# A RWKV scan in double periods: the triangular solver moved to GpSimd one period ahead, and transfers, norms and weight splits set in another order

## The chip, the core and the metric

The kernel runs on one core of a Trainium2 chip. A core has five engines with a queue each: PE (TensorE, matrix multiplication), DVE (VectorE), ACT (ScalarE), POOL (GpSimd) and SP (SyncE, which here only starts DMA transfers). The metric is the device time of one execution in microseconds (us). Before the change three runs gave 2839.25, 2841.23 and 2844.28 us; the median is 2841.23.

## What is computed

A decoder trunk of two layers over 272 tokens (16 learned ones and 256 of the input) with 2048 channels, in float32. Layer 0 mixes tokens by RWKV-7 with 32 heads of 64 channels, then has a SwiGLU block; layer 1 has stick-breaking attention and another SwiGLU block. The change touches layer 0's mixing alone:

```python
r = xr @ w_r;  k = xk @ w_k;  v = xv @ w_v
w = -softplus(-(dec_w0 + tanh(xw @ dec_w1) @ dec_w2)) - 0.5
decay = exp(-exp(w))
a = sigmoid(a_w0 + (xa @ a_w1) @ a_w2)
g = sigmoid(xg @ g_w1) @ g_w2
kk = heads(k * k_k);  kk = kk * rsqrt(max(sum(kk * kk), 1e-24))
k = k * (1 + (a - 1) * k_a)
def step(state, inp):                       # one token, for each head
    sa = einsum('bhvk,bhk->bhv', state, -kk_t)
    state = state * d_t + sa * (kk_t * a_t) + v_t * k_t
    return state, einsum('bhvk,bhk->bhv', state, r_t)
y = group_norm(y) * gn_w + gn_b             # over each head
out = ((y + sum(r * k * r_k) * v) * g) @ w_o
```

## The kernel before

**Stages.** `prologue` normalizes the tokens, computes all of k and the hidden layers of the low-rank products, and prepares the mixed inputs of r and v. `scan` (L662) runs the recurrence and, beside it, the projections of r and v and the first part of the output projection. The SwiGLU blocks and the attention follow; they are not touched.

**Pairs and chunks.** Two heads make a pair of 128 channels; there are 16 pairs. A pair's 272 tokens are a chunk of 16 and four chunks of 64. Within a chunk the recurrence is a triangular system, so a chunk needs the inverse of a unit triangular 64 x 64 matrix built from the scores `An` (L1323). The inverse is made in two stages. First its 16 x 16 diagonal blocks: the scores go to a DRAM scratch `s1` (L1308), from where a transfer picks the diagonals of two pairs into `As` on 80 partitions (`diagonals`, L826); `solve` (L832) inverts them all by 14 steps of two DVE operations; `inverse` (L848) writes the result `Ts` to a scratch `s2` and reads it back as the tile `Tt`. Then `left` and `right` (L1382, L1405) double the blocks, once for size 16 and once for 32, by TensorE. `apply`, `trans` and `states` (L1420, L1436, L1456) turn the inverse into chunk transitions, and `step` (L1471) walks through the four chunks.

**The double period.** `scan` works on two pairs at a time, in turn d = -2 to 7. In each turn, A is the pair of pairs at its end (states, steps, group norm, gate), B the one in its middle (scores, inverse, transitions), and C the one at its start: `lora` (L1199) makes decays and the scaled key tensors of one pair from the low-rank products. N is the one behind C, for which weights are loaded. In one turn, the order before the change is: A's states and steps with B's `neg` and `chunk0` between them; B's scores and `diagonals`; `bonus`, `tokens`; A's norm, one pair after the other; `solve`; C's first `lora`; `values`; A's gates; `inverse`; left 16, C's second `lora`, right 16, left 32, right 32, apply, trans.

**Fill.** Between these parts stand calls `f(k)`: they draw k steps from `stream` (L902), each three matmuls of 272 columns for the r and v projections (w_v before w_r; 64 steps per turn). The weights come in 512 KB tiles `raw` on SyncE's queue (four buffers), are split into `whi` by ACT and `wlo` by DVE in parts of 512 columns, four steps each (`whl_pair`, L222; six buffers), and `chunks` (L857) splits one part ahead of its use.

**Order.** TensorE's and SyncE's instructions keep the order of the program text. For the other engines the framework's scheduler orders them by its own estimate of when operands are ready, unless the text pins an instruction: `in_step` (L820), `issue_after` and the manual dependencies in `chunks` do so before the change. Each engine runs its queue in order, and a wait holds up all behind it.

**Queues.** `self.dq` (L391) gives pair 0 of a turn SyncE's queue for its scratch transfers, and pair 1 GpSimd's. `load_low` and `split_low` (L788, L802) load and split the small second-stage weights: one pair's decay weights together with another pair's gate weights, and with the former the tile `rn`, the reciprocal norms of the keys. GpSimd computes most of `lora`'s products (`E` in L1202), among them kk, the product of the keys with `rn`.

**Buffers.** `BUFS` (L54) lists how many buffers a tag has; a tag that is not listed has one, and `ALIAS` (L38) lets two names share a tag.

Of the kernel before, what the change touches and what calls it, by code (L numbers as in the profile page):

```python
# [18 lines left out]
NK = D // 128  # L19
# [18 lines left out]
ALIAS = {"kk": "ld", "rs2": "L", "rk": "Q", "Ah": "Tn", "Mp": "Ys", "sq": "ta"}  # L38
# [15 lines left out]
BUFS = {n: 2 for n in "ARV BK AR0 G An Tt X BV0 Tn Ys Rh S KV0 WV0 y bv hs rn".split()}  # L54
BUFS.update(bv=3, pe=6)

# [75 lines left out]
class Builder:  # L132
# [240 lines left out]
    def time_mix(self):  # L373
# [15 lines left out]
        with ExitStack() as ctx:  # L389
            sp = ctx.enter_context(tc.tile_pool(name="sp", bufs=1, reuse_waits="tile"))  # L390
            self.dq = nc.sync, nc.gpsimd  # L391
            self.static = []
            self.s2 = []
# [3 lines left out]
            for i in range(2):  # L397
                st = {}
                for n, w in (("B0", 64), ("V0", 64), ("SC0", 128)):
                    st[n] = sp.tile([128, w], F32, name=f"{n}_{i}", tag=f"{n}_{i}")  # L400
                    nc.gpsimd.memset(st[n], 0.0)
                self.static.append(st)
                z = self.dram.tile([10, 65, 64], F32, name=f"s2_{i}", tag=f"s2_{i}", bufs=1)
                nc.scalar.dma_start(z.rearrange("s i t -> (s i t)").rearrange("(p x) -> p x", p=128),
                                  zero)
                self.s2.append(z)
# [255 lines left out]
    def scan(self, sp):  # L662
# [24 lines left out]
        self.load_low(None, pairs[0])  # L687
        for d in range(-2, NK // 2):
            A, B, C, N = two(d), two(d + 1), two(d + 2), two(d + 3)
            f = fill if C else lambda k: fill(k * 7 / 8)  # L690
            self.split_low(nth(A, 0), nth(C, 0), self.latest)
            self.load_low(nth(A, 1), nth(C, 1))
            if d == -2:
                C[0].lora(4, 5)
                f(12)
                pop, head_sq, key_max, key_norm = self.late_keys
                head_sq(*pop())
                late = key_max(1)
                f(28)
                self.split_low(None, C[1], self.steps[-1])  # L700
                self.load_low(None, N[0])
                C[1].lora(0, 1)
                f(24)
                continue
# [3 lines left out]
            for c in range(1, 5):  # L708
                for x in A:
                    x.step(c)  # L710
                if not B:
                    fill(1)
                elif c < 3:
                    B[c - 1].neg()
                elif c == 3:
                    if not A:
                        f(6)
                    for x in B:
                        x.chunk0()
# [5 lines left out]
            if B:  # L725
                B[0].bonus()
            for x in B:
                x.tokens()
            if A:
                A[0].square()  # L730
                A[0].variance()
            f(2)
            if A:
                A[0].norm()
            if B:
                B[1].bonus()
            if A:
                A[1].square()
            f(2)
            if A:  # L740
                A[1].variance()
            f(2)
            with tc.issue_after(self.solve(B).ins) if B else nullcontext():
                if A:
                    A[1].norm()
                if C:
                    C[0].lora(2, 3)
                f(4)
                if A or C:
                    self.split_low(nth(A, 1), nth(C, 1), self.steps[-1])  # L750
                    self.load_low(nth(B, 0), nth(N, 0))
                f(4)
                for x in B:
                    x.values()
                f(4)
                if A:
                    A[0].gate()
                f(4)
                if A:
                    A[1].gate()  # L760
                f(6 if A else 4)
            if B:
                self.inverse(B)
            for x in B:
                x.left(16)
            f(5)
            if C:
                C[1].lora(0, 1)
            for x in B:
                x.right(16)  # L770
            f(5)
            for x in B:
                x.left(32)
            f(5)
            for x in B:
                x.right(32)
            if d == -1:
# [10 lines left out]
    def load_low(self, A, C):  # L788

        if not (A or C):  # L790
            return
        nc, a = self.nc, self.a
        self.low = self.l2.tile([128, 512], F32, name="w2", tag="w2", bufs=2)
        if C:
            p = C.p
            nc.sync.dma_start(self.low[:, :256], a["lora2"][p][:, :256])
            C.rn = C.t272("rn")
            nc.sync.dma_start(C.rn, self.rkd[2 * p:2 * p + 2].unsqueeze(1).to_broadcast([2, 64, T]))
        if A:
            nc.sync.dma_start(self.low[:, 256:], a["lora2"][A.p][:, 256:512])  # L800

    def split_low(self, A, C, after):  # L802
        c = slice(0 if C else 256, 512 if A else 256)
        h = self.l2.tile([128, 512], F32R, name="w2h", tag="w2h", bufs=1)
        l = self.l2.tile([128, 512], F32R, name="w2l", tag="w2l", bufs=1)
        hi = self.nc.scalar.copy(h[:, c], self.low[:, c])
        if after:
            nosync = mybir.DependencyInfo(mybir.DependencyClass.NoSync, mybir.DependencyReason.DATA)
            self.tc.add_manual_dep(hi.ins, after.ins.name, nosync,
                                   reason="weights that land late")  # L810
        self.nc.vector.tensor_tensor(l[:, c], self.low[:, c], h[:, c].bitcast(F32), ALU.subtract)
        for x, o, r in (C, 0, 96), (A, 256, 128):
            if x:
                x.w2 = [(h[:r, i:i + 128], l[:r, i:i + 128]) for i in (o, o + 128)]
# [5 lines left out]
    def in_step(self, op):  # L820

        nosync = mybir.DependencyInfo(mybir.DependencyClass.NoSync, mybir.DependencyReason.DATA)
        self.tc.add_manual_dep(op.ins, self.steps[-1].ins.name, nosync,
                               reason="operands that land late")

    def diagonals(self, two):  # L826

        self.As = self.sp.tile([80, 16, 16], F32, name="As", tag="As")
        for i, x in enumerate(two):
            self.dq[i].dma_start(self.As[i * 40:i * 40 + 40], x.diag(x.s1))  # L830

    def solve(self, two):  # L832
# [4 lines left out]
        self.in_step(V.tensor_tensor(Ts.rearrange("p i t -> p (i t)"), As.rearrange("p i t -> p (i t)"),  # L837
                                     self.cst("eye16")[:80], ALU.add))
        for i in range(1, 15):
            n = 15 - i  # L840
            t = Tm[:, :i * n].rearrange("p (i t) -> p i t", t=n)
            V.tensor_tensor(t, Ts[:, 0:i, i:i + 1].to_broadcast([80, i, n]),  # L842
                            As[:, i:i + 1, i + 1:].to_broadcast([80, i, n]), ALU.mult)
            op = V.tensor_tensor(Ts[:, 0:i, i + 1:], Ts[:, 0:i, i + 1:], t, ALU.add)  # L844
        self.Ts = Ts
        return op

    def inverse(self, two):  # L848
        for i, x in enumerate(two):
            self.dq[i].dma_start(x.diag(self.s2[i]), self.Ts[i * 40:i * 40 + 40])  # L850
        for i, x in enumerate(two):
            x.Tt = x.big("Tt", 5, 64)
            s2 = self.s2[i].rearrange("(a r) i t -> r i a t", r=2)
            for r in range(2):
                self.dq[i].dma_start(x.Tt[HS[r]], s2[r, 0:64])

    def chunks(self, jobs):  # L857
# [17 lines left out]
        nosync = mybir.DependencyInfo(mybir.DependencyClass.NoSync, mybir.DependencyReason.DATA)  # L875
        count = [0]
        self.steps = []
# [693 lines left out]
```

## Time and profile before

| what | us |
|---|---|
| median of three runs | 2841.23 |
| the profiled execution | 2843.48 |
| its span, first to last instruction | 2841.7 |
| TensorE busy | 2671.2 (94%) |
| VectorE busy | 1802.2 (63%) |
| ScalarE busy | 1491.4 (52%) |
| GpSimd busy | 211.7 (7%) |

The page's strip cuts the span into 40 slices of 71 us and gives the busy share of each engine in tenths. The stretches outside the scan show 9 for TensorE; the scan lies in slices 3 to 11. Matmul records are pipelined and overlap, so a busy TensorE is not one at its peak; how far apart matmuls start tells more. A row of a timeline has the start, the duration, engine, line, operation, and in brackets the idle time before and what ended it. A row of the waits has the total, the count and the longest.

### The profile page before, as it was taken

What the parts mean: (1) busy time and instruction counts of PE and PEld (TensorE: products, weight loads), DVE (VectorE), ACT (ScalarE), POOL (GpSimd) and SP (SyncE); (2) the same over time, 40 slices, a digit from 0 to 9 for tenths busy, and PEclk for the clock granted to TensorE, in tenths of its full rate; (3) what the DMA queues carried; (4) which work ended last, traced back from release to release, by engine and by line L of the source; (5) the groups of instructions that cost most, each with busy time, mean ns of one, the idle gap of its engine ahead of it and who ended that gap; (6) DMA issues with size and microseconds to landing.
All of it is one profiled execution on the core that took longest, in us unless ns stands there. A gap on an engine that the chain in (4) does not pass through costs nothing.

```text
span 2841.7 us, 54127 instructions
## 1 busy us (share of the span) xinstructions
PE 2671.2 (94%) x20966; PEld 2494.3 (88%) x20966; DVE 1802.2 (63%) x3689; ACT 1491.4 (52%) x3016; POOL 211.7 (7%) x301
## 2 busy tenths in 40 slices
PE   9987677768799999999999999999999999999999
PEld 8887667667699999999999999988888888888888
DVE  7665445556566555555555777578876666666666
ACT  7764443445465444444444576467655455455554
POOL 0033233333200000000000000000000000000000
PEclk9998888888899999999999999999999999999999
DMA  6442322232445555555555555543455565655655
GB/s 228 129 118 76 83 83 70 74 83 68 119 149 173 173 176 179 162 188 176 166 186 173 164 183 167 175 148 116 148 186 188 178 199 178 199 187 177 201 182 175
DMA packets 168146, 439.57 MB, mean 155 GB/s; under 512 B 38544, under 2 KB 70704, under 8 KB 167888
## 3 DMA queue, kind: packets, MB, share of 16 engines
q1 hardware_dynamic: 164240, 429.62, 48.1%
q0 software_dynamic: 3072, 5.53, 0.9%
q8 instruction: 164, 2.69, 0.4%
q10 hardware_dynamic: 576, 0.96, 0.1%
q14 instruction: 94, 0.77, 0.1%
HBM read 430.28 MB, written 5.74 MB: 153 GB/s over the span
## 4 chain that ended last, share of the span: by engine, by line
PE 87%; DMA 4%; DVE 3%; POOL 2%; ACT 2%; issue 1%; SPq 1%; DVEq 0%; POOLq 0%; ACTq 0%
PE mm L204 21%; PE mm L199 15%; PE mm L201 15%; PE mm L200 15%; PE mm L203 11%; DMA s<-Ts 2%; PE lr L598 1%; PE mm L499 1%; POOL k L1227 1%; DVE Tm L842 1%; DVE Ts L844 1%; PE yb L1394 1%; DMA Tt<-s 1%; PE zb L1410 1%; PE wa L1427 1%
## 5 line engine op out<-in xcount | busy, mean ns | idle before, releaser
L181 DVE TENSOR_TENSOR wlo<-raw,whi 128x512 fp32r<-128x512 f32 (+1 forms) x1432 | 968.2, 679 | 593.2 <-ACT whi L180 575.0
L180 ACT CAST whi<-raw 128x512 fp32r<-128x512 f32 (+1 forms) x1432 | 870.0, 610 | 839.6 <-PE mm L200 528.0
L199 PE MATMUL mm<-hl,whi 128*128 128x272 f32 x3328 | 975.7, 293 | 0.2 <-ACT whi L227 0.2
L200 PE MATMUL mm<-hl,whi 128*128 128x272 f32 x3328 | 969.3, 291 | 5.0 <-DVE hl L271 5.0
L201 PE MATMUL mm<-hl,wlo 128*128 128x272 f32 x3328 | 970.6, 292 | 0.2 <-DVE wlo L228 0.2
L204 PE MATMUL mm<-hl,whi 128*128 128x512 f32 x2624 | 919.7, 394 | 0.0
L203 PE MATMUL mm<-hl,wlo 128*128 128x256 f32 x2624 | 738.0, 282 | 0.0
L200 PEld LDWEIGHTS mm<-hl,whi 128*128 128x128 f32 x3328 | 642.5, 193 | 5.5 <-DVE hl L271 5.4
L199 PEld LDWEIGHTS mm<-hl,whi 128*128 128x128 f32 x3328 | 637.2, 191 | 5.1 <-issue 0.5
L201 PEld LDWEIGHTS mm<-hl,wlo 128*128 128x128 f32 x3328 | 636.8, 191 | 0.7 <-DVE wlo L228 0.4
L204 PEld LDWEIGHTS mm<-hl,whi 128*128 128x128 f32 x2624 | 492.4, 188 | 111.9
L203 PEld LDWEIGHTS mm<-hl,wlo 128*128 128x128 f32 x2624 | 494.3, 188 | 0.3
L227 ACT CAST whi<-raw 128x512 fp32r<-128x512 f32 (+1 forms) x154 | 92.5, 612 | 186.1 <-PE mm L200 119.1
L228 DVE TENSOR_TENSOR wlo<-raw,whi 128x512 fp32r<-128x512 f32 (+1 forms) x154 | 113.3, 754 | 110.6 <-ACT whi L227 107.3
L1394 PE MATMUL yb<-Tt,An 64*64 64x64 f32 x512 | 28.7, 260 | 84.4 <-DMA Tt<-s 84.2
L1394 PEld LDWEIGHTS yb<-Tt,An 64*64 64x64 f32 x512 | 24.3, 169 | 88.8 <-issue 79.3
L220 DVE TENSOR_TENSOR h<-h,mm 128x256 f32<-128x256 f32 (+1 forms) x224 | 93.9, 420 | 6.6 <-PE mm L204 6.0
L201 PE MATMUL mm<-hi,wlo 128*128 128x272 f32 x256 | 77.2, 302 | 21.1 <-DVE wlo L228 21.1
L199 PE MATMUL mm<-hi,whi 128*128 128x272 f32 x256 | 78.8, 308 | 0.0
L213 ACT COPY c<-mm 128x256 f32<-128x256 f32 x104 | 38.8, 373 | 76.0 <-PE mm L204 76.0
L200 PE MATMUL mm<-lo,whi 128*128 128x272 f32 x256 | 75.8, 296 | 0.0
L201 PEld LDWEIGHTS mm<-hi,wlo 128*128 128x128 f32 x256 | 50.6, 198 | 22.6 <-DVE wlo L228 22.6
(303 smaller groups left out, 2502.3 us busy)
## 6 DMA issues: line engine op xcount, KB each, us to landing
raw<-w_gate SPq DMA_DIRECT2D x176, 512.0 KB
raw<-w_up SPq DMA_DIRECT2D x176, 512.0 KB
raw<-w_down SPq DMA_DIRECT2D x128, 512.0 KB
raw<-w_down SPq DMA_DIRECT2D x128, 192.0 KB
raw<-w_v SPq DMA_DIRECT2D x32, 512.0 KB
raw<-w_r SPq DMA_DIRECT2D x32, 512.0 KB
raw<-sb_w_k SPq DMA_DIRECT2D x32, 512.0 KB
raw<-sb_w_v SPq DMA_DIRECT2D x32, 512.0 KB
```

The costliest lines, as they stand in the source:

```text
L180: nc.scalar.copy(hi, part)
L181: nc.vector.tensor_tensor(lo, part, hi.bitcast(F32), ALU.subtract)
L199: mm(out, w[0], x[0], start=first, stop=False)
L200: mm(out, w[0], x[1], start=False, stop=False)
L201: return mm(out, w[1], x[0], start=False, stop=last)
L203: mm(out[:, :n], w[1], x[0], start=first, stop=False, skip_group_check=True)
L204: return mm(out, w[0], x[2], start=False, stop=last, skip_group_check=True)
L213: self.nc.scalar.copy(c, out[:, n:])
L220: self.nc.vector.tensor_tensor(h, h, out[:, c:c + n], ALU.add)
L227: self.cast = nc.scalar.copy(hi, part)
L228: nc.vector.tensor_tensor(lo, part, hi.bitcast(F32), ALU.subtract)
L1394: PE.matmul(yb[r, i * 64:i * 64 + 64], An[r, i], Tt[r, i], start=True, stop=True)
```

## The change

- The scratch transfers of both pairs go on SyncE's queue (`self.dq`); `s1` becomes a fixed pair of tiles, zeroed once, like `s2`.
- `neg` moves to a new place, behind right 32, and works for C, the pairs that are B in the next turn. It also computes chunk 0's negative scores, into a new tile `An0`. Behind it, in the new function `negatives`, stand `diagonals`, which now writes `An` and `An0` (the scores in transposed form) to `s1`, and `solve`, which runs on GpSimd, over a transposed view of `As`, in 15 steps of two operations on a copy of the identity.
- `inverse` stands behind B's `tokens`; A's `square`, `variance`, the new `log` and `norm` follow for both pairs together.
- `lora` of both C pairs uses banks 2 and 3 and stands at other places. kk and the four products with it move from GpSimd to DVE, as fused operations.
- `load_low` and `split_low` serve the two pairs of C; `load_gates` and `split_gates` those of A. `rn` gets its own `load_norm` and has one buffer; `bv` has four.
- w_r comes before w_v. Parts are split three ahead (`AHEAD`), each cast from the 13th on pinned behind what the text has put on ACT before it. `step` is cut into `update` and `output`.

The order of the turn, cut to its core:

```diff
-            self.split_low(nth(A, 0), nth(C, 0), self.latest)
-            self.load_low(nth(A, 1), nth(C, 1))
+            gates = self.load_gates(A)
+            if C:
+                self.split_low(C)
             for x in A:
                 x.states()
             for c in range(1, 5):
                 for x in A:
-                    x.step(c)
+                    x.update(c)
+                for x in A:
+                    x.output(c)
-                elif c < 3:
-                    B[c - 1].neg()
+                elif c < 3:
+                    B[c - 1].chunk0()
             for x in B:
                 x.scores()
-            if B:
-                self.diagonals(B)
             f(6 if A else 2)
+            for x in B:
+                x.bonus()
             for x in B:
                 x.tokens()
-            (A[0] square, variance, f(2), norm; B[1].bonus; A[1] the same)
-            with tc.issue_after(self.solve(B).ins) if B else nullcontext():
-                (A[1].norm, C[0].lora, splits and loads, values, gates)
             if B:
                 self.inverse(B)
+            for x in A:
+                x.square()
+            for x in A:
+                x.variance()
+            for x in A:
+                x.log()
+            for x in A:
+                x.norm()
+            f(4)
+            if C:
+                C[0].lora(2, 3)
+            f(4)
             for x in B:
                 x.left(16)
             f(5)
-            if C:
-                C[1].lora(0, 1)
             for x in B:
                 x.right(16)
+            for x in B:
+                x.values()
+            if C:
+                C[1].load_norm()
             f(5)
+            if C:
+                C[1].lora(2, 3)
+            f(5)
+            self.split_gates(gates, A)
+            f(4)
+            for x in A:
+                x.gate()
             for x in B:
                 x.left(32)
-            f(5)
+            f(7)
             for x in B:
                 x.right(32)
+            if C:
+                self.negatives(C)
-            f(5)
+            f(8)
             for x in B:
                 x.apply()
-            f(5)
+            if N:
+                self.load_low(N)
+                N[0].load_norm()
+            f(8)
             for x in B:
                 x.trans()
-            f(5)
+            f(8)
```

The transfers and the solver:

```diff
     def diagonals(self, two):
         self.As = self.sp.tile([80, 16, 16], F32, name="As", tag="As")
         for i, x in enumerate(two):
-            self.dq[i].dma_start(self.As[i * 40:i * 40 + 40], x.diag(x.s1))
+            s1 = self.s1[i].rearrange("(a r) i t -> r i a t", r=2)
+            for r in range(2):
+                self.dq.dma_start(s1[r, 0:64, 0:4], x.An[HS[r]])
+                self.dq.dma_start(s1[r, 0:META, 4, 0:META], x.An0[HS[r]][:META])
+        for i, x in enumerate(two):
+            self.dq.dma_start(self.As[i * 40:i * 40 + 40], x.diag(self.s1[i]))
...
-        V, As = self.nc.vector, self.As
+        V, As = self.nc.gpsimd, self.As.rearrange("p t i -> p i t")
...
-        for i in range(1, 15):
+        for i in range(15):
             n = 15 - i
-            t = Tm[:, :i * n].rearrange("p (i t) -> p i t", t=n)
-            V.tensor_tensor(t, Ts[:, 0:i, i:i + 1].to_broadcast([80, i, n]),
-                            As[:, i:i + 1, i + 1:].to_broadcast([80, i, n]), ALU.mult)
-            op = V.tensor_tensor(Ts[:, 0:i, i + 1:], Ts[:, 0:i, i + 1:], t, ALU.add)
+            t = Tm[:, :(i + 1) * n].rearrange("p (i t) -> p i t", t=n)
+            V.tensor_tensor(t, Ts[:, 0:i + 1, i:i + 1].to_broadcast([80, i + 1, n]),
+                            As[:, i:i + 1, i + 1:].to_broadcast([80, i + 1, n]), ALU.mult)
+            V.tensor_tensor(Ts[:, 0:i + 1, i + 1:], Ts[:, 0:i + 1, i + 1:], t, ALU.add)
```

In `neg`, and in `lora`'s products:

```diff
+        for h in HS:
+            self.PE.matmul(b0[0][h, 128:128 + META][:META], self.AR0[h, 0], self.B0[h, 0:META],
+                           start=True, stop=True)
+        self.An0 = An0 = self.big("An0", META)
+        for h in HS:
+            self.A.copy(An0[h][:META], b0[0][h, 128:128 + META][:META])
...
-        E.tensor_scalar(kk, kt, self.vec("k_k"), -1.0, ALU.mult, ALU.mult)
-        E.tensor_tensor(kk, kk, rn, ALU.mult)
+        V.scalar_tensor_tensor(kk, kt, self.vec("k_k"), rn, ALU.mult, ALU.mult)
```

The splits and their order:

```diff
-            if 12 < count[0] <= 30:
-                self.tc.add_manual_dep(self.cast.ins, self.steps[4 * (count[0] - 4) + 3].ins.name,
-                                       nosync, reason="splits in step with their use")
+            if count[0] > 12:
+                self.tc.keep_in_program_order(self.cast)
...
-                w = split(raws[i], k, min(k + 4, j1 - j0))
+                ahead.append(split(raws[i], k, min(k + 4, j1 - j0)))
                 if k + 4 >= j1 - j0:
                     load()
-                if ahead:
-                    yield from ahead
-                ahead = w
+                if len(ahead) > AHEAD:
+                    yield from ahead.pop(0)
```

More of the change, by code (lines that the diff above doesn't have):

```diff
@@ L686, in scan @@
         self.latest = None
-        self.load_low(None, pairs[0])
+        self.load_low(two(0))
+        pairs[0].load_norm()
         for d in range(-2, NK // 2):
@@ L816, in bank, with split_gates @@
+    def split_gates(self, w, two):
+        if not two:
+            return
+        h, l = self.whl_pair(w)
+        self.tc.keep_in_program_order(self.cast)
+        for i, x in enumerate(two):
+            x.wg = [(h[:, o:o + 128], l[:, o:o + 128]) for o in (i * 256, i * 256 + 128)]
     def bank(self, i, name):
         return self.pbank.tile([128, 512], F32, name=name, tag=f"b{i}")
[L820 to L824, printed above, removed]
@@ L912, in stream @@
         for p in range(NK):
-            for acts, done in (self.xv, pairs[p].after_v), (self.xr, pairs[p].after_r):
+            for acts, done in (self.xr, pairs[p].after_r), (self.xv, pairs[p].after_v):
                 out = self.mmbank()[:, :T]
```

208 lines of the change are left out of this document (89 added, 119 removed).

## The prediction

> **What bounds the kernel now.** I read the strip of the page first: TensorE is at nine tenths everywhere but in slices 3 to 11, about 160 to 800 us. That is the RWKV scan, and all that the diff touches. The table of stretches, cut at the first left step of each double period, shows what one period costs there.
>
> ```profile
> core 0: us, PE busy (x) PEld busy (x) DVE busy (x) ACT busy (x) POOL busy (x), PEclk, DMA share, GB/s
> 225.60:303.50 77.90, 54.64 (x723) 50.30 (x724) 41.71 (x110) 34.60 (x82) 27.18 (x34) 0.87 0.29 78
> ...
> 381.70:459.60 77.90, 56.39 (x720) 52.45 (x720) 39.72 (x107) 33.89 (x80) 25.78 (x34) 0.83 0.28 76
> ...
> 616.20:687.70 71.50, 58.09 (x736) 53.93 (x736) 41.75 (x111) 34.84 (x82) 26.10 (x34) 0.86 0.31 89
> 687.70:757.90 70.20, 52.57 (x683) 48.50 (x683) 40.00 (x110) 34.75 (x82) 23.23 (x38) 0.83 0.34 92
> ```
>
> Five periods take 78.1 us on average (225.6 to 616.2), then 71.5 and 70.2. No engine is full: DVE is at 51%, ACT at 44%, POOL at 33%. So waits set the period. TensorE's waits in 381.6 to 459.7:
>
> ```profile
> PE yb L1394 <- DMA Tt<-s: 13.5, 3, 13.1
> PE vb L1190 <- DVE bv L1339: 5.8, 1, 5.8
> PE mm L201 <- DVE wlo L228: 2.4, 1, 2.4
> ```
>
> A wait costs twice. TensorE's own timeline, just behind the 13.1 us wait before (its left step at 381.67) and then in a steady part:
>
> ```profile
> 384.41 0.43 PE L199 MATMUL mm<-hl,whi 128*128 128x272 f32 x1
> 384.64 0.43 PE L200 MATMUL mm<-hl,whi 128*128 128x272 f32 x1
> ...
> 389.37 0.29 PE L199 MATMUL mm<-hl,whi 128*128 128x272 f32 x1
> 389.50 0.29 PE L200 MATMUL mm<-hl,whi 128*128 128x272 f32 x1
> ...
> 390.50 0.28 PE L199 MATMUL mm<-hl,whi 128*128 128x272 f32 x1
> ```
>
> Matmuls start 0.23 us apart behind the gap, 0.126 us in the steady part; a fill step (three matmuls) is (390.50 - 389.37)/3 = 0.377 us. The granted clock of the period is 0.83, so a third of it (0.17 x 2 x 78 = 26 us) is at half clock; 21.3 us of that is about the waits themselves, and some 13 us of work runs at half speed (the clock falls only a little after a gap begins), which loses 6.6 us. Without waits the period would be 78.1 - 21.3 - 6.6 = **50 us**.
>
> Why is Tt late? SyncE's queue goes in program order:
>
> ```profile
> 418.20 0.42 SPq L796 DMA_DIRECT2D w<-lora  x1
> 443.95 0.55 SPq L798 DMA_DIRECT2D rn<-rkd  x1
> ...
> 445.11 0.84 SPq L872 DMA_DIRECT2D raw<-w_r  x2
> 446.06 0.37 SPq L872 DMA_DIRECT2D raw<-w_v  x1
> 446.48 0.50 SPq L850 DMA_DIRECT2D s<-Ts  x1
> 456.40 1.27 SPq L855 DMA_DIRECT2D Tt<-s  x2
> ```
>
> ```profile
> SPq L798 <- POOL AR L1252: 26.0, 2, 25.6
> ```
>
> ```profile
> 433.62 0.88 POOL L850 DMA_DIRECT2D s<-Ts  x1 [13.19 <-DVE ld L1213]
> ```
>
> The solver was done by 433; the other pair's copy left from POOL at 433.62. SyncE sat 25.6 us on the load of rn, whose buffer GpSimd still read, then had three 512 KB loads to issue, and its copy of Ts, issued at 446.48, landed behind them:
>
> ```profile
> 446.48 9.87 DMA s<-Ts
> ...
> 457.06 2.51 DMA Tt<-s
> ```
>
> So the wait is a queue's order, not the solver's length.
>
> **The change part by part.** *Order on SyncE.* The copy of Ts and the reads of Tt now stand ahead of the rn loads and the loads of the next fill steps. The 25.6 us block no longer lies before them. What is late next is the solver itself, which now has a chain of its own from the new place of neg (behind right(32)) to left(16) of the next period. I set its length against TensorE's work between the two.
>
> *TensorE's distance.* From left(16) to neg in program order: 26 fill steps, 9.8 us; one lora (6 matmuls) and two gates (12), 2.3 us at 0.126; left and right twice and values, five blocks of some 1.2 us, of which the longest, right(32), is this:
>
> ```profile
> 394.35 0.68 PE L1410 MATMUL zb<-Ys,Tn 64*64 64x64 f32 x16
> ...
> 395.66 0.39 PE L199 MATMUL mm<-hi,whi 128*128 128x272 f32 x1
> ```
>
> It takes 1.3 us from start to start; with some 1 us of changeovers the sum is **19 us**. The rest, 50 - 19 = **31 us**, is what TensorE has to do while the chain runs.
>
> *The chain.* neg's 32 score matmuls and a few for chunk 0, and ACT's copies: 2 us. Then four transfers a pair, all on SyncE:
>
> ```profile
> 413.03 0.61 SPq L1310 DMA_DIRECT2D s<-G  x1
> 413.69 0.61 SPq L1312 DMA_DIRECT2D s<-SC  x1
> ```
>
> ```profile
> As<-s POOLq DMA_DIRECT2D x8, 40.0 KB, 4.5
> ...
> s<-SC POOLq DMA_DIRECT2D x16, 16.0 KB, 2.2
> ```
>
> ```profile
> L830 POOL DMA_DIRECT2D As<-s x8: 905/914/931, 197.0 to 726.2; - x8
> ```
>
> About 0.65 us each to issue: pair 0 ends at 4.6, lands at 6.8. The new tile An0 is not in the table of buffers, so it has one; pair 1's copy into it waits for pair 0's transfers out of it. Add 0.4 for ACT, three issues and a landing: 11.4. The read of As, 0.3 to issue and some 3 to land (4.5 less POOL's own 0.91, rounded down): **14.7 us**.
>
> The solver has 15 x 2 operations and a copy. DVE did 14 x 2 in about 0.2 us each:
>
> ```profile
> L842 DVE TENSOR_TENSOR Tm<-Ts,As x112: 170/200/634, 200.9 to 741.0; 80x14 f32<-80x14 f32 x16, 80x26 f32<-80x26 f32 x16, 80x36 f32<-80x36 f32 x16, 80x44 f32<-80x44 f32 x16
> ```
>
> GpSimd's price for such shapes is not in the trace. The nearest rows:
>
> ```profile
> L1259 POOL TENSOR_TENSOR B<-k,Q x16: 215/224/668, 164.7 to 700.7; 128x16 f32<-128x16 f32 x16
> ```
>
> ```profile
> L1232 POOL TENSOR_TENSOR kk<-kk,rn x16: 762/773/1195, 162.8 to 697.7; 128x272 f32<-128x272 f32 x16
> ```
>
> ```profile
> 440.37 0.07 issue
> 440.44 0.78 POOL k L1228
> ```
>
> From 16 to 272 elements: 2.14 ns each on 224 ns. The sizes k(16-k), k = 1 to 15, have a mean of 45, so 0.287 us; with 0.07 us between dependent operations (the chain of waits, just quoted) 30 x 0.36 + 0.4 = 11.2 us. That is the lower end: the strided, broadcast operands and DVE are not in it. Upper end, the slowest small operation (0.668) every time: 22 us. I take **14.5**, nearer the median rows. Sum: 29.2.
>
> Then two copies of Ts (0.5 each), the first landing about 2 us after its issue (extrapolated from POOL's), two Tt reads of 0.6 and 2.5 to land: 6 us for pair 0, 0.8 more for pair 1 where pair 0's left does not hide it. Sum: 36. Weight loads are on the same queue: three cost 9.87 - 2 = 8, so 2.6 each; I count one over the four hops. **Chain 38.6 us**, against 31: TensorE still waits **7.6 us** at left(16), and then runs 5 us at half clock, which loses 2.4. Period: 50 + 7.6 + 2.4 = **60 us**.
>
> *Variance and norms.* Both squares now come behind both bonus sums, the variances together behind tokens, and both logs ahead of both exponentials.
>
> ```profile
> L1498 ACT ACT_TABLE_LOAD x2 | 2.6, 1283 | 0.0
> ```
>
> Four table loads a period become two: 2.6 us of ACT. The 5.8 us wait was for the second variance behind the first one's norm on DVE; that order goes. DVE has 4 G and 4 bv operations and 2 subtractions (some 5 us) to do under the 6 us of fill, bonus and tokens. I leave 0.5 us of wait for it in the rounding of 60.
>
> *Splits three chunks ahead.* Twelve steps, 4.5 us of cover, against a 2.4 us wait: gone. Each cast is now held behind the ACT work traced before it; if ACT is stuck there over 4.5 us, the matmuls wait. Cost at nothing, bounded by 2.4 us a period.
>
> *DVE and GpSimd.* DVE loses the solver (5.9 us) and gains six operations a pair (some 2.3 us a pair); GpSimd gets 14.5 and gives up eight operations and its DMAs. Neither fills 60 us. The rn tile goes to one buffer, but its loads wait for DVE's kk, early in lora, not for a chain on GpSimd. The gate weights' two loads move ahead, under cover.
>
> **Sum**, against the profiled run's own 2843.48 (span 2841.7): five periods, 5 x (78.1 - 60) = 90; the next two, 11.5 and about 12 (70.2 against 58, with 7/8 of the fill); first left step unmoved at 225.6 (the same chain stands before it, and no rn block); end, two variances and table loads in one, 4. Together 118: 2725. The median of the shown runs is 2 us under the profiled one. **Predicted: 2725 us.**
>
> **Rivals.** (a) *The chain is hidden.* If the solver takes 11 us, the transfers meet no load and the two pairs' An0 overlap, the chain is 31 or less and the period 51 to 53: 7 x about 25 + 5 = 180 less, 2665 at best. For it: only 7 us are missing. Against: eight serial issues on one queue.
>
> (b) *The chain is longer.* Solver at its upper end, 22 us, and two loads ahead of it: 49, period 70 to 71: 5 x 7.5 and a little, 2795 to 2800.
>
> (c) *GpSimd is kept out; slower.*
>
> ```profile
> 435.56 4.80 POOL L1227 TENSOR_SCALAR k<-ta,vecs,dv 128x272 f32<-128x272 f32 x1 [1.06 <-ACT ta L1216]
> ```
>
> ```profile
> 437.44 2.47 DVE L228 TENSOR_TENSOR wlo<-raw,whi 128x512 fp32r<-128x512 f32 x4
> ```
>
> ```profile
> L1227 POOL TENSOR_SCALAR k<-ta,vecs,dv x16: 568/989/4812, 159.8 to 694.5; 128x272 f32<-128x272 f32 x16
> ```
>
> ```profile
> L1227 POOL TENSOR_SCALAR k<-ta,vecs,dv 128x272 f32<-128x272 f32 x16 | 38.2, 2386 | 131.8 <-ACT ta L1216 131.8
> ```
>
> This operation takes 0.57 us at best; here it ended 0.45 us after DVE's run of splits did. Each of the solver's 30 gaps lets DVE in again. If every second operation met a wait of L1227's mean (2.39 us), the solver would take 15 x 2.39 + 15 x 0.36 = 41 us, the chain 65, the period 86: 7 x 9 or more slower, about 2910. It decides from 1.0 to 1.2 us an operation on (chain 56, period 78). Against: DVE is busy half of the period and gets no new work in the window, so it can take about 8 us out of 15, not 26; other POOL rows stay within 0.1 us of their medians (773 against a minimum of 762). The Trainium skill, "SBUF — State Buffer", section "Who interferes with whom", says that a DVE instruction with two SBUF inputs shuts out a GpSimd instruction that reads SBUF, whole instruction by whole instruction. The trace agrees for L1227; by that rule alone (c) would have more weight than I give it.
>
> (d) *It doesn't do what it says:* SyncE stalls elsewhere (at As or rn) and the weight loads are late, period still near 78: within 10 us of before.
>
> **Chances.** Forecast, period 56 to 66 (2685 to 2765): 0.52. (a) 0.2, (b) 0.16, (c) 0.08, (d) 0.04. The range reaches to (a)'s 2665 and (b)'s 2795, and leaves out (c) and (d) and the tails. A measurement of this kernel can tell about 0.2% from no change; faster by more 0.88, same 0.03, slower 0.09.
>
> **What would show it.** First, TensorE's wait for Tt: 5 to 10 us a period. Near 0 speaks for (a). Second, the solver's operations on POOL: 0.4 to 0.5 us each. Third, no wait of SyncE over 10 us for rn; its longest should be for POOL's Ts. Fourth, vb under 1.5 us, two table loads a period. Fifth, pair 1's An0 copy on ACT behind a DMA. The forecast is wrong if the solver's mean leaves 0.36 to 0.7 us, or if a wait for wlo or whi, which I put at nothing, takes Tt's place.

## The result, and the profile after

The changed kernel takes 2765.97 us (median of 4 runs, 2764.34 to 2768.93), the kernel before in the same comparison 2841.92 (2839.25 to 2844.28). The ratio is 0.9734, with a 95% interval of 0.9717 to 0.9751. The forecast was 2725, the range 2665 to 2795: the sign and the range held, the place of the time that is left did not, and the time lies just above the 2685 to 2765 that the forecast gave its own case.

The table of stretches of the changed kernel, cut at its first left(16) of each double period (left(16) is the left step for size 16; PEclk is the granted TensorE clock, 1.00 being full speed):

```profile
core 0: us, PE busy (x) PEld busy (x) DVE busy (x) ACT busy (x) POOL busy (x), PEclk, DMA share, GB/s
213.40:265.90 52.50, 50.00 (x714) 45.64 (x714) 27.96 (x72) 27.07 (x73) 14.10 (x39) 1.00 0.42 114
...
465.80:531.60 65.80, 54.33 (x729) 50.05 (x728) 36.70 (x90) 30.68 (x83) 16.57 (x41) 0.92 0.34 89
...
597.70:671.90 74.20, 58.08 (x718) 53.39 (x717) 43.72 (x106) 35.35 (x96) 25.18 (x56) 0.84 0.36 104
```

The first period, in which no pair has come to its norm yet, takes 52.5 us at a clock of 1.00 (53.2 from the start of its left step, 212.74). The next five take 66.3 each (265.93 to 597.65), the last 74.3. Seven periods take 459.2 us instead of 531.5 (225.67 to 757.19 before). The first left step starts 12.9 us earlier (212.74), and what follows the start of the last one takes 2095.3 us instead of 2084.5: left(16) now stands at 14 fill steps of its program period, not at 34, so 20 steps of 0.377 us, 7.5 us, moved from before the first left step to behind the last.

TensorE's longest waits of the whole run, in the table of waits (total, times, longest):

```profile
PE zb L1418 <- DVE Tn L1394: 40.9, 6, 6.9
PE gp L202 <- DVE wlo L229: 18.3, 6, 3.7
PE cb L1493 <- ACT S L1487: 9.8, 22, 3.5
...
PE vb L1193 <- ACT hs L1198: 2.7, 2, 2.2
```

The wait for Tt, 13.1 us a period, is gone, and so is the wait for bv. A new one stands one stage later: right(16) waits 6.9 us for Tn, the transposed Tt, and the gates' products 2.9 for wlo. VectorE's timeline at that place, with left(16) at 465.81:

```profile
465.80 0.79 DVE L1517 TENSOR_TENSOR t<-rs 128x272 f32<-128x272 f32 x2 [4.14 <-ACT rs L1516]
...
468.83 1.41 DVE L1521 SCALAR_TENSOR_TENSOR y<-y,dv,bv 128x272 f32<-128x272 f32 x2
470.17 0.68 DVE L229 TENSOR_TENSOR wlo<-raw,whi 128x512 fp32r<-128x512 f32 x1
...
470.98 0.41 DVE L1407 TENSOR_TENSOR Ys<-yb,consts 128x256 f32<-128x256 f32 x1
...
475.04 0.41 DVE L1263 TENSOR_TENSOR BK<-kk,Q 128x256 f32<-128x256 f32 x1
475.37 0.76 DVE L1394 STREAM_TRANSPOSE Tn<-Tt 128x256 f32<-128x256 f32 x2
```

Tn needs only Tt, which has been there since left(16). But VectorE runs in one fixed order, and in it Tn, which the change pins at its place in the text (L1396), stands behind two norms, which wait for ScalarE's exponential, and behind the first pair's whole low-rank part. TensorE has its left step and five fill steps done by 469 and then stands still:

```profile
475.95 1.65 PE L1418 MATMUL zb<-Ys,Tn 64*64 64x64 f32 x26 [6.89 <-DVE Tn L1394]
```

The chain that the forecast was about, one period on (queue of SyncE; neg's first matmul is at 498.23, the next left(16) at 531.63):

```profile
499.57 0.61 SPq L834 DMA_DIRECT2D s<-An  x1
...
504.11 0.30 SPq L835 DMA_DIRECT2D s<-An  x1
...
505.85 1.33 SPq L837 DMA_DIRECT2D As<-s  x2
...
521.33 0.83 SPq L855 DMA_DIRECT2D s<-Ts  x2
525.79 3.46 SPq L860 DMA_DIRECT2D Tt<-s  x4
```

GpSimd's solver runs between them, from 509.00 to 521.26:

```profile
509.00 0.63 POOL L848 TENSOR_TENSOR Tm<-Ts,As 80x15 f32<-80x15 f32 x1 [23.01 <-PE rm L1451]
509.71 0.21 POOL L850 TENSOR_TENSOR Ts<-Ts,Tm 80x15 f32<-80x15 f32 x1
...
521.03 0.23 POOL L850 TENSOR_TENSOR Ts<-Ts,Tm 80x15 f32<-80x15 f32 x1
```

So the chain is at most 33.4 us from neg to left(16), of which the solver is 12.3, and TensorE has about as much work in between: the chain has just gone out of sight.

SyncE no longer stands 25.6 us on rn. Its largest waits in the scan, each summed over the run, are for buffers of the weight loads and for the copies of An; those ahead of the copy of Ts (L855), which the forecast put first, make 19.0 us in all:

```profile
SPq L877 <- DVE wlo L229: 131.3, 29, 9.6
SPq L834 <- ACT An L1335: 61.9, 8, 10.3
```

### The profile page after: what moved, and what is told of

It reads as the page before. It is cut to its first block, busy times and chain, and to the rows that moved or that the text cites. A ratio compares the mean times of both kernels' runs of the same rounds, so it can differ in the third digit from the quotient of the medians.

```text
span 2767.2 us, 54183 instructions
## 1 busy us (share of the span) xinstructions
PE 2664.3 (96%) x21030; PEld 2484.6 (90%) x21030; DVE 1780.0 (64%) x3549; ACT 1468.1 (53%) x3030; POOL 144.5 (5%) x357
## 4 chain that ended last, share of the span: by engine, by line
PE 87%; DVE 5%; ACT 3%; DMA 2%; issue 2%; POOL 1%; SPq 0%; DVEq 0%; ACTq 0%; POOLq 0%
PE mm L205 22%; PE mm L200 15%; PE mm L202 15%; PE mm L201 15%; PE mm L204 11%; DMA rn<-rkd 1%; PE lr L601 1%; PE mm L502 1%; DVE wlo L229 1%; PE zb L1418 1%; PE cb L1493 1%; PE z L1122 1%; PE lt L1135 0%; PE yb L1402 0%; POOL Tm L848 0%
## 5 line engine op out<-in xcount | busy, mean ns | idle before, releaser
L1418 PE MATMUL zb<-Ys,Tn 64*64 64x64 f32 x512 | 24.4, 256 | 42.3 <-DVE Tn L1394 40.9
L1418 PEld LDWEIGHTS zb<-Ys,Tn 64*64 64x64 f32 x512 | 21.7, 167 | 45.2 <-issue 42.3
L200 PEld LDWEIGHTS mm<-hi,whi 128*128 128x128 f32 x256 | 50.2, 196 | 2.9 <-issue 0.6
```

What stands on the lines that cost most here:

```text
L200: mm(out, w[0], x[0], start=first, stop=False)
L1418: self.PE.matmul(zb[r, i * 64:i * 64 + 64], self.Tn[r, i], self.Ys[r, i], start=True, stop=True)
```

## The experiments

The medians of the table are of 4 runs. "Period" is the mean of the second to the sixth period (75.9 in the kernel before, from 302.81 to 682.42). The medians of the kernel before lay between 2840.9 and 2842.9 in the comparisons.

| run | median us | ratio to before (95%) | period us |
|---|---|---|---|
| changed kernel | 2766.0 | 0.9734 (0.9717 to 0.9751) | 66.3 |
| tn_early | 2751.5 | 0.9678 (0.9663 to 0.9692) | 63.1 |
| tn_early_an0 | 2747.3 | 0.9664 (0.9649 to 0.9678) | 63.0 |
| solve_twice | 2824.9 | 0.9938 (0.9923 to 0.9953) | 72.2 |
| rn_later (on before) | 2813.7 | 0.9899 (0.9883 to 0.9916) | 73.4 |
| rn_later_sp (on before) | 2783.6 | 0.9794 (0.9779 to 0.9809) | 66.6 |
| dve_solver | 2782.0 | 0.9793 (0.9778 to 0.9807) | 68.1 |
| ahead1 | 2816.3 | 0.9912 (0.9898 to 0.9927) | 72.5 |
| pin30 | 2734.3 | 0.9622 (0.9605 to 0.9639) | 61.1 |
| norm_late_rn | 2719.5 | 0.9568 (0.9552 to 0.9584) | 59.0 |
| bank01 | 2699.4 | 0.9497 (0.9482 to 0.9512) | 55.6 |
| bank01_dve | 2705.8 | 0.9519 (0.9504 to 0.9534) | 57.3 |
| bank01_pin30 | 2708.2 | 0.9526 (0.9510 to 0.9542) | 57.2 |

The theory at the start: what is left of the period is VectorE's order, not the solver's chain. The rival: the chain is as long as the period, and with Tn out of the way Tt would be late again.

**Tn early** (tn_early). The two transposes get a place of their own ahead of the norms.

```diff
-            for x in A:
-                x.norm()
+            turn = None
+            for x in B:
+                turn = x.turn()
+            with tc.issue_after(turn.ins) if B else nullcontext():
+                for x in A:
+                    x.norm()
...
+    def turn(self):
+        flat = "p c t -> p (c t)"
+        self.Tn = self.big("Tn", 4, 64)
+        op = self.V.transpose(self.Tn.rearrange(flat), self.Tt[:, :4].rearrange(flat))
+        return self.b.tc.keep_in_program_order(op)
```

> The two transposes of Tn(16) are traced ahead of the norms of the next pairs, so that VectorE's fixed order no longer has them behind the last low-rank operation of the same period. Theory (VectorE's queue sets the period): the wait zb <- DVE Tn of 6.9 us a period goes, some 2 to 3 us stay for Ys, which still stands behind the norms; the period falls from 66 to between 58 and 62 us, the total by 25 to 50 us to 2716 to 2741. Rival (the chain of the solver is as long as the period): the chain starts earlier by what the period shrinks, TensorE comes to left(16) before Tt has landed, a wait yb <- Tt of 3 to 7 us appears in place of the other, and the total falls by less than 15 us.

Measured: 14.5 us less than the changed kernel. The wait for Tn is gone, Ys stays late by the expected 2.5 us, and no wait for Tt comes (the whole run has 2.1 us of it, the changed kernel 1.7). The table of waits:

```profile
PE gp L202 <- DVE wlo L229: 21.5, 6, 4.5
PE zb L1427 <- DVE Ys L1416: 19.2, 14, 2.5
PE gp L200 <- ACT whi L228: 7.4, 6, 1.9
...
PE yb L1411 <- DMA Tt<-s: 2.1, 3, 1.4
```

The theory had the kind right and the size wrong by half: Ys, and then the gate weights, are later in the same queue, and take over part of the wait. The total fits the rival's (less than 15 us), but the wait for Tt that the rival rests on is not there.

**An0 in two buffers** (tn_early_an0).

```diff
-BUFS.update(bv=4, pe=6)
+BUFS.update(bv=4, pe=6, An0=2)
```

> The same, and An0 has two buffers, so that the second pair's copy of An0 does not wait for the first pair's transfer out of it. Theory (VectorE's queue sets the period): within 0.3% of the run with Tn early alone, since the chain ends in time anyway. Rival (chain): the chain is shorter by the 2 to 4 us by which that copy waited, a wait yb <- Tt shrinks by the same, and the total is 10 to 20 us below the run with Tn early alone.

Measured: 4.2 us less than with Tn early alone, the period the same (63.0 and 63.1). As the theory has it, the chain ends in time anyway. The ranges of the two overlap (2747.7 to 2754.2 and 2745.5 to 2748.5), so whether the 4 us are real isn't settled.

**A longer solver** (solve_twice). 30 more multiplications and two more operations, which add zero.

```diff
+            for _ in range(2):
+                V.tensor_tensor(t, Ts[:, 0:i + 1, i:i + 1].to_broadcast([80, i + 1, n]),
+                                As[:, i:i + 1, i + 1:].to_broadcast([80, i + 1, n]), ALU.mult)
...
+        V.tensor_tensor(Tm[:, :16], Tm[:, :16], Tm[:, :16], ALU.subtract)
+        V.tensor_tensor(Ts[:, 0:1, 0:1], Ts[:, 0:1, 0:1], Tm[:, 0:1].unsqueeze(1), ALU.add)
```

> The solver runs 32 more operations on GpSimd that change nothing, which at 0.36 to 0.41 us each lengthen the chain from neg to left(16) by 11 to 13 us. Theory (the chain has only just come out of sight, with 33 us against TensorE's own way of about the same length): Tt lands late at left(16) by 8 to 12 us; the wait zb <- Tn that stood behind it shrinks by the same, up to its 6.9 us, so that the period grows by 2 to 6 us and the total by 15 to 40 us. Rival (the chain has 10 us or more of room): no wait for Tt and a total within 0.3% of the changed kernel's 2766.

Measured: 58.9 us more. TensorE's waits from 506 to 577.5 us, one period:

```profile
PE yb L1410 <- DMA Tt<-s: 7.8, 2, 7.5
...
PE zb L1426 <- DVE Tn L1402: 1.5, 1, 1.5
```

The solver takes 25 us now (548.14 to about 573.3), 13 more. Tt is late by 7.5 to 8, so some 5 of the 13 us are absorbed. Not all of that is room of the changed kernel's chain: here the read of Tt is issued 2.1 us behind the copy of Ts (573.38 to 575.49 on SyncE's queue), there 4.5 (521.33 to 525.79). Tn's wait shrinks by 5.4 and the period grows by 5.9, as the theory said. The total is above the expected 15 to 40, since the expectation left out the start: the first left step moves by 12.1 us and the first period, which has no wait for Tn to give back, grows by 11.3. These and 5 x 5.9 + 7.7 for the last period make 60. The rival is out.

**The queue before the change** (rn_later, on the kernel before). The load of rn goes out of load_low, and the next pair's is issued behind the inverse.

```diff
-            C.rn = C.t272("rn")
-            nc.sync.dma_start(C.rn, self.rkd[2 * p:2 * p + 2].unsqueeze(1).to_broadcast([2, 64, T]))
...
+            if N and d > -2:
+                N[0].load_norm()
```

> The kernel before, with one thing changed: the load of the norm weights rn of the next pair is issued behind the inverse of the pair in hand, not at the head of SyncE's queue ahead of the raw loads and the copy of Ts. Theory (a queue's order made Tt late, not the length of the solver): the wait yb <- Tt of 13.1 us a period falls to under 4, the period from 78 to about 66 us, the total by 50 to 75 us to 2767 to 2792, so most of the gain of the change without moving the solver. Rival (the solver on VectorE, or the wait for bv, sets the period): Tt is as late as before or vb <- bv grows to the same length, and the total stays within 20 us of 2842.

Measured: 28.3 us less than before; neither guess. The first pair's wait of 13.1 us fell to 1.8, but then the second pair's came out, 5.7 us. Its read of Tt is on GpSimd's queue, behind the low-rank operations:

```profile
427.37 0.77 POOL L1236 TENSOR_TENSOR k<-k,kt 128x272 f32<-128x272 f32 x1
...
433.79 0.74 POOL L1266 TENSOR_TENSOR BK<-kk,Q 128x256 f32<-128x256 f32 x1
434.47 1.47 POOL L859 DMA_DIRECT2D Tt<-s  x2
```

**Both pairs on SyncE** (rn_later_sp, on top of rn_later).

```diff
-            self.dq = nc.sync, nc.gpsimd
+            self.dq = nc.sync, nc.sync
```

> The kernel before with its rn load moved, and with the transfers of both pairs on SyncE's queue; in the run with rn alone the second pair's read of Tt was issued on GpSimd's queue at 434.5 us, behind twelve low-rank operations of GpSimd, and TensorE waited 5.7 us a period for it. Theory (only queues made Tt late, SyncE's for the first pair, GpSimd's for the second; the solver on VectorE is short enough): the wait of 5.7 us falls under 1.5, the period from 73.4 to 66 to 69 us, the total from 2814 to 2770 to 2790. Rival (both pairs' copies now stand behind the raw loads on SyncE's queue): both Tt come late by 3 us or more, and the total stays within 10 us of 2814.

Measured: 57.3 us less than before, period 66.6. The waits for Tt of the whole run were 84.2 us before and 48.4 with rn_later; now they are these:

```profile
PE yb L1402 <- DMA Tt<-s: 18.6, 22, 4.5
```

A left step still waits 0.4 to 4.7 us, mostly a little more than the expected 1.5. So two queues made Tt late, and with both put right the old kernel, its solver still on VectorE, gets 57 of the change's 76 us. What it keeps besides, in the period from 422.9 to 488, are the 5.9 us for bv and 2.9 for wlo.

**The solver back on VectorE** (dve_solver).

```diff
-        V, As = self.nc.gpsimd, self.As.rearrange("p t i -> p i t")
+        V, As = self.nc.vector, self.As.rearrange("p t i -> p i t")
```

> The changed kernel with the solver's 31 operations on VectorE in place of GpSimd, all else as it is. Theory (the solver's engine matters because VectorE's fixed order is what the period waits for): the 7.1 us of solver come on top of VectorE's 36.7 us a period, splits and hs behind them are late, waits for wlo or vb of 3 to 6 us a period appear on TensorE, and the total is 20 to 45 us over the changed kernel's 2766. Rival (the queues of the transfers were the matter, the engine was not): the chain is 5 us shorter, no new wait appears, and the total stays within 8 us of 2766.

Measured: 16.0 us more than the changed kernel, between the two. Two periods in the table of stretches:

```profile
540.40:610.60 70.20, 58.00 (x729) 53.43 (x728) 43.23 (x121) 30.89 (x83) 6.29 (x10) 0.85 0.32 84
474.20:540.40 66.20, 53.99 (x729) 49.70 (x728) 42.73 (x122) 30.80 (x83) 6.19 (x10) 0.92 0.33 89
```

VectorE has 42.7 us of work in the second row instead of 36.7, and the period is as long as in the changed kernel: its queue has the room. The profiled execution, 10.2 us longer than that of the changed kernel, loses time in some periods only (the first 55.9 instead of 53.2, the second 70.9 instead of 66.8, the sixth, in the first row, 70.2 instead of 66.0), and its last is shorter (70.9 instead of 74.3). In the sixth the waits of cb for S are 2.2 us instead of 1.0, but in the second row, which isn't longer, they are 1.8; what differs there is the granted clock, 0.85 against 0.92. Why it falls isn't shown.

**Splits one step ahead** (ahead1).

```diff
-AHEAD = 3
+AHEAD = 1
```

> The changed kernel with weight splits traced one step ahead of their use in place of three. Theory of the forecast (the splits' distance removes 2.4 us of waits for wlo a period, and some half clock behind them): waits mm <- wlo of 2 to 5 us a period come back, and the total is 15 to 35 us over 2766. Rival (the wait zb <- Tn of 6.9 us stands behind them and gives the same time back): the new waits shorten that one, and the total is within 8 us of 2766.

Measured: 50.3 us more. The table of waits:

```profile
PE mm L202 <- DVE wlo L229: 48.0, 28, 3.7
PE mm L200 <- ACT whi L228: 43.9, 28, 3.7
```

That is 13 us of waits a period. The wait for Tn gives back its 6.9 and the gates theirs, 3.5: the rival's mechanism is there, but its total is out, and the theory's 15 to 35 is passed as well. The forecast's term of 2.4 a period was far too small for this kernel.

**Casts free from the 31st on** (pin30).

```diff
-            if count[0] > 12:
+            if 12 < count[0] <= 30:
```

> The changed kernel with the casts of the weight splits held in program order for the 13th to the 30th alone, as before, in place of all from the 13th. Theory (in the period from 597.7 to 671.9 us a cast held in order waits 2.7 us for its raw load and holds ScalarE up, and cb waits 3.5 us for S behind it): that period falls from 74 to 70 to 72 us, the others are as they were, and the total is 0 to 6 us less. Rival (the order keeps the splits ahead of their use in every period): waits for whi or wlo come back, and the total is 10 us or more above 2766.

Measured: 31.6 us less, in all periods from the second on (61.1), not in the last alone. Both guesses missed. With the casts free VectorE's planned order is another. Its timeline, with left(16) at 450.61:

```profile
445.68 0.45 DVE L1394 STREAM_TRANSPOSE Tn<-Tt 128x256 f32<-128x256 f32 x1 [1.59 <-DMA Tt<-s]
...
456.13 0.42 DVE L1394 STREAM_TRANSPOSE Tn<-Tt 128x256 f32<-128x256 f32 x1
...
457.27 0.42 DVE L1259 SCALAR_TENSOR_TENSOR ARV<-kk,P 128x256 f32<-128x256 f32 x1
```

One Tn is ahead of the norms, the other ahead of kk and its products. TensorE's waits in the period from 450.6 to 510.2:

```profile
PE yb L1402 <- DVE o L1530: 2.4, 1, 2.4
PE zb L1418 <- DVE Ys L1407: 1.9, 1, 1.9
...
PE zb L1418 <- DVE AR L1258: 0.8, 1, 0.8
```

zb waits 2.7 us instead of 6.9, the gates nothing instead of 3.5, and left(32), the other yb, now waits 2.4 for the gated output o. Why the planner chose so isn't shown.

**Norms behind Ys** (norm_late_rn), on top of tn_early_an0.

```diff
+            with tc.issue_after(last.ins) if B else nullcontext():
+                for x in A:
+                    x.norm()
...
                 C[0].lora(2, 3)
+                C[1].load_norm()
...
+            self.split_gates(gates, A)
             if C:
                 C[1].lora(2, 3)
             f(5)
-            self.split_gates(gates, A)
```

Here `last` is the second pair's Ys of left(16), and only the VectorE part of the norm moves; the exponential stays where it was. The run makes three moves at once, so their shares aren't told apart.

> On top of Tn early and An0 in two buffers: the VectorE part of both norms stands behind the two Ys, the second rn load is issued right behind the first pair's low-rank part, and the gate weights are split ahead of the second pair's low-rank part. Theory (the waits that are left in the period, zb <- Ys 2.5 us, gp <- wlo 3.0 and gp <- whi 1.2, come from that fixed order): zb <- Ys falls under 0.5, gp <- wlo and whi under 1.5 together, the period from 63 to between 56 and 60 us, the total from 2747 to 2712 to 2735. Rival (the chain, some 4 us of room): left(16) comes 4 us earlier or more against neg and waits 2 to 4 us for Tt; the total stays above 2738.

Measured: 2719.5 us, period 59.0, as the theory said. The waits for Ys, wlo and whi are gone, none for Tt comes. Left(32) waits 1.6 us for o, and one longer wait is left:

```profile
453.42 0.59 PE L200 MATMUL zw<-dec_w1h,w2h 96*128 96x272 f32 x1 [3.96 <-DVE Tt L1434]
```

The second pair's zw has the PSUM bank that zb has, and VectorE adds zb to Tt behind the norms.

**Other banks for it** (bank01).

```diff
-                C[1].lora(2, 3)
+                C[1].lora(0, 1)
```

> On top of the run norm_late_rn: the second pair's low-rank products go to PSUM banks 0 and 1 in place of 2 and 3, which right(16) holds until VectorE has added zb to Tt, behind the norms. Theory (that is the period's last wait, zw <- DVE Tt 4.0 us): it goes, at most 1.5 us of waits for the banks 0 and 1 take its place, the period falls from 59 to between 55 and 57 us and the total from 2720 to 2696 to 2710. Rival (the copies of kv and k out of banks 0 and 1 stand behind the first pair's exponentials on ScalarE, or Tt now comes late): zw waits as long for ScalarE, or yb for Tt, and the total stays above 2714.

Measured: 2699.4 us, ratio 0.9497 (0.9482 to 0.9512), the best version of the study: 67 us under the changed kernel. The period from 431.9 to 487.5:

```profile
431.90:487.50 55.60, 51.85 (x729) 47.05 (x728) 37.00 (x90) 30.46 (x83) 15.44 (x41) 1.00 0.40 106
```

Its longest wait is 0.7 us and the clock is 1.00. VectorE does the same 37 us of work as in the changed kernel (36.7); what differs is its order, with the second pair's banks and An0's second buffer.

**The same with the solver on VectorE** (bank01_dve), and **with the casts free** (bank01_pin30).

> The run bank01 with the solver on VectorE. In the changed kernel that cost 16 us, a part of it hidden in the wait for Tn. Theory (GpSimd is worth little by itself): 10 to 20 us over bank01. Rival (with its other waits gone the period is VectorE's, so 7 us of solver each period are seen): 30 to 50 us over bank01.

> The run bank01 with the casts held in program order from the 13th to the 30th alone, as in the run pin30, which was 32 us below the changed kernel. Theory (freeing the casts only put Tn and the gate weights' split elsewhere in VectorE's order, which bank01 does by name): the gains do not add, and the total is within 8 us of bank01's 2699. Rival (the casts held in order cost ScalarE time of their own): another 10 to 30 us less, 2670 to 2690.

Measured: 6.5 us more than bank01 with VectorE's solver, less than either guess, nearest the theory that GpSimd is worth little by itself. With the casts free 8.8 us more, not less: the gain of pin30 does not add, so holding the casts costs nothing as long as VectorE's order is named. Left(32) waits for o again, up to 2.4 us, as in pin30. The expected bound of 8 us is just missed.

## Why the prediction was right, and where it was wrong

- *Waits set the period; the wait for Tt is a queue's order, not the solver's length.* Right, shown by rn_later_sp. But SyncE's block on rn was only the half of it: rn_later alone gave 28 us, and the other half was the second pair's read behind GpSimd's low-rank operations. The forecast quoted the other pair's copy on GpSimd's queue at 433.62, and did not follow that pair to its read of Tt.
- *Five periods of 78.1, then 71.5 and 70.2.* Some of these stretches are cut at the second pair's left step, where it waits by itself (687.7, the first pair's being at 682.42): from first step to first step they are 78.0, 66.8 and 74.8, with nearly the same sum.
- *Wait-free period 50 us.* Some 2 to 3 us low: the first period takes 52.5 at full clock, and bank01's 55.6 less its waits (3.5 us) is 52.1.
- *TensorE's distance 31 us.* About right: 33.4 from neg to left(16), with no wait over 1 us in it.
- *Chain 38.6 us.* Oversized. To the solver's start it was 10.8 us (498.23 to 509.00), not 14.7: the second pair's copy of An0 ran behind the first pair's transfers (ScalarE's row below), yet that cost little. The solver took 12.3, not 14.5: 0.41 us an operation with its gap, near the lower end of 0.36. So *TensorE still waits 7.6 us for Tt* fell, and the signpost of 5 to 10 us read near 0, which the forecast had named as speaking for rival (a). From the solver's end to left(16) there are 10.4 us, no less than the 9.4 that the forecast had for the last four hops. solve_twice puts the room at 5 us at most.

```profile
503.93 0.34 ACT L1338 COPY An<-b 16x16 f32<-16x16 f32 x2
```

- *Neither fills 60 us*, said of VectorE and GpSimd, **is the step that failed**. It is true of the sum (VectorE 36.7 us of 65.8) and says nothing of the order. Tn, pinned, came to stand behind two norms that now end together and behind a low-rank part that used to be on GpSimd: 6.9 us of wait, and 2.9 + 0.6 for the gate weights, where nothing was counted. The gates' wait for wlo and whi is the forecast's own last sign of being wrong, come true in part. norm_late_rn and bank01 show the price with the same work on VectorE: 66.3 falls to 55.6. This put the period at 66 instead of 60, and it is most of why rival (a) did not come out at its 2665 though the chain was hidden; even bank01, without these waits, stays 34 us above that.
- *Splits three chunks ahead: 2.4 us a period, gone.* The wait is gone, the term was too small: in the changed kernel, whose casts are pinned, ahead1 costs 6.2 us a period and 50 in all.
- *Casts held in order, cost at nothing, bounded by 2.4.* The bound broke: 5.2 us a period (pin30). The way goes through VectorE's order rather than ScalarE: bank01_pin30, where that order is named, gains nothing from free casts. How the casts move that order isn't shown.
- *Variances and norms.* Right: the 5.8 us for bv went, two table loads a period are left, and vb waits 2.2 us once.
- *First left step unmoved, end 4 us earlier.* Wrong by 12.9 and 14.8, which nearly cancel.
- *Rival (c), GpSimd kept out.* It did happen, on four of 30 operations (below); at 0.41 us each the solver is far from the 1.0 where it decides.

In the sum: five periods gave 71.1 us instead of 90, the next two 1.3 instead of 23.5, start and end together some 2 instead of 4. That the total lay in the range is in part luck: the two errors, a chain too long and an order unseen, work against each other.

## What to carry to other kernels

An engine that is half idle can still set the period, when its instructions run in one fixed order: for each operation that the critical engine needs, read what stands ahead of it in that order, not how busy the engine is. When a long wait goes, look for the next operation that stands behind long ones in the same order, and price the change with that. A queue's DMA order has to be followed for every pair and every queue; putting the order right on both queues brought most of the gain without moving the solver.

## What the runs showed of the hardware

VectorE did hold GpSimd up, for one operation at a time. GpSimd's solver in the changed kernel:

```profile
510.99 0.26 POOL L850 TENSOR_TENSOR Ts<-Ts,Tm 80x39 f32<-80x39 f32 x1
511.32 0.62 POOL L848 TENSOR_TENSOR Tm<-Ts,As 80x48 f32<-80x48 f32 x1
512.03 0.28 POOL L850 TENSOR_TENSOR Ts<-Ts,Tm 80x48 f32<-80x48 f32 x1
```

and VectorE beside it:

```profile
510.86 0.28 DVE L1458 TENSOR_TENSOR Rh<-rm,Rh 128x128 f32<-128x128 f32 x1
511.05 0.74 DVE L229 TENSOR_TENSOR wlo<-raw,whi 128x512 fp32r<-128x512 f32 x1
```

The operation that began under wlo (two operands in SBUF) took 0.62 us instead of about 0.3 and ended just behind it; those beside Rh<-rm,Rh (one operand in PSUM) took 0.21 to 0.28. Four of the 30 in this period were hit so (509.00, 511.32, 514.32, 520.29), some 1.5 us together. The Trainium skill, "SBUF — State Buffer", section "Who interferes with whom", has this rule, with a VectorE instruction of at most one SBUF input left out of it, and the trace agrees on both sides.

The granted clock is lower in periods with long waits, but the waits' lengths alone do not set it. With waits of 6.9 and 2.9 us in the period it is 0.92, and in bank01, with none over 0.7, 1.00; but the two rows of dve_solver, with 6.9 and 2.9 us in the one and 6.9 and 2.4 in the other, have 0.92 and 0.85. Behind the 3.96 us wait of norm_late_rn (TensorE's timeline) matmuls start 0.23 us apart until 456.76, for 3.3 us, and 0.126 after that:

```profile
456.31 0.43 PE L200 MATMUL mm<-hl,whi 128*128 128x272 f32 x1
456.53 0.40 PE L201 MATMUL mm<-hl,whi 128*128 128x272 f32 x1
456.76 0.30 PE L202 MATMUL mm<-hl,wlo 128*128 128x272 f32 x1
...
457.27 0.29 PE L200 MATMUL mm<-hl,whi 128*128 128x272 f32 x1
457.39 0.29 PE L201 MATMUL mm<-hl,whi 128*128 128x272 f32 x1
```
